# A transformer step on one core: the second branch's values as seven products of a pair, with the caches, the sums of x and the norm buffers moved

## The chip, the cores and the metric

The kernel runs on one core of a Trainium2 chip. The metric is the device time of one execution in microseconds (us), as the median of several runs. A core has five engines that run beside one another and meet through semaphores: TensorE (PE, matmuls and transposes), VectorE (DVE), ScalarE (ACT), GpSimd (POOL) and SyncE (SP, which here issues most DMA transfers). Each engine takes its instructions strictly in the order in which the program wrote them.

## The reference

One layer of a hybrid encoder, for 1024 prompt tokens and 64 sample tokens of width 1024, in float32:

```python
h = rms_norm(x, norm_w) @ w_in            # 6144 columns
sb_q, sb_k, sb_v, sb_z, cb_q, cb_k, cb_v, cb_z, g_sb, g_cb = split(h)
cb_q = rms_norm(cb_q per head, q_norm_w); cb_k = rms_norm(cb_k per head, k_norm_w)
o_sb = stick_breaking(sb_q, sb_k, sb_v)   # 8 heads x 64, all earlier keys
#   A[t,s] = beta[t,s] * prod_{s<j<t} (1 - beta[t,j]), beta = sigmoid(q.k/8)
o_cb = band_attention(cb_q, cb_k, cb_v, rel_bias)   # 8 heads x 64, a band of 512 and a bias
b_sb = (o_sb * silu(sb_z)) @ w_proj_sb;  b_cb = (o_cb * silu(cb_z)) @ w_proj_cb
y = x + (sigmoid(g_sb) * b_sb + sigmoid(g_cb) * b_cb) @ w_out
```

The sample tokens do the same against caches of 512 keys and values per branch. Beside y the kernel returns the new keys and values of both branches; of the second branch's prompt tokens, the last 512.

## The kernel before

Every float32 operand is split into a high part and a rest, both held in the rounded format F32R (`hi` and `lo` in the code). A product is three matmuls for each slice of 128 of the contracted dimension: high by high, rest by high, high by rest. ACT makes the high part as a copy, DVE or POOL the rest as a subtraction.

The projection by `w_in` comes first, in two stages.

The first stage (lines 202 to 577) works in natural layout, tokens on the partitions: for columns that need it, namely values (`sbv` from column 1024, `cbv` from 3072) and the second branch's queries and keys (from 2048 and 2560), which are normed per head. The list `NB` names eight blocks of 256 columns, `TO` the nine token tiles: the 64 sample tokens as tile 8 first, then tiles 0 to 7 of 128 tokens. The loop at line 492 takes block `i`, tile `ti`: 24 matmuls of 256 columns into an accumulator `acc` (16 for the sample tile, whose high part and rest lie side by side as 128 rows; `fold` adds the halves). Accumulators come from `psF` (two) and `psA` (one, every third tile). `evac_nat` empties one: for values ACT copies it to `vst`, which SP stores to the scratch `d_sbv` or `d_cbv` and to the output; for queries and keys ACT copies it to `qn` and squares it, DVE sums the squares and POOL raises them to a power (`rsqrt`), and a tile later `norm_nat` multiplies on DVE twice. `pend` holds normed tiles; when three wait, `post_nat` transposes the oldest on PE into the one PSUM tile `pk`, ACT makes its high part `hl`, DVE the rest.

Between the tiles of this loop stand, at places given as (block, tile), the other jobs. During the first block `ready` prepares x itself: `prep_s` (mean square), `prep_a` (`xn`, DVE), `prep_b` (transposes into `pt`, then `xa`, `xm`, `xb`). `W.split` makes the next block's weights: copy on ACT, subtraction on POOL (line 124); `load_nat` loads the ones after. `cache_load` loads a key cache into `ck`, and `cache_pair` transposes one of its four head pairs: four transposes on PE into the one PSUM tile `pc`, copy to `hc` on ACT, subtraction on DVE, one store of 512 KB to `d_csbT` or `d_ccbT`; `hc` has one buffer. `load_rb` loads the bias table into the buffer of `ck`, `make_rb` makes one head's reversed bias row `rx` on DVE and stores it to `d_rb`. `make_t` (line 162) makes four sums of x, four slices each, as 16 steps: two or three additions of 544 columns on DVE give `d`, then ACT copies and DVE subtracts (`put_t`).

The order on every engine is the one in which this code writes the instructions out; a pool that is closed gives its memory to the next one, whose first writes wait for the last readers, DMA reads among them.

The second stage (lines 582 to 732) takes the remaining columns in pairs of 128, tokens along the free dimension, by seven products for eight (Strassen's scheme in Winograd's form): two halves of x's tokens by two halves of its features against two by two weight quarters. It uses the sums of x from `make_t` (`tms`) and sums of weights from `presum`; `prep(n)` makes the weights of product n, copy on ACT and subtraction on POOL, five products ahead. Attention and the output follow and aren't touched by the change.

## Time and profile before

| | |
|---|---|
| Median of 3 runs (lowest to highest) | 967.85 us (967.75 to 968.23) |
| The profiled execution's own time | 967.6 us |
| Its span | 965.8 us |
| Busy: PE / DVE / ACT / POOL | 957.4 / 592.0 / 475.9 / 395.1 us |
| DMA traffic, mean rate | 175.76 MB, 182 GB/s |
| First matmul of the second stage | 226.6 us after the start |

A row of the timeline gives the start and the duration of an instruction in us, its engine, its line in the kernel, its operation, output and inputs, its shape, and in brackets how long its engine stood idle before it and what it then waited for. Groups give a count and durations in ns. A matmul's duration reaches from its issue to its end; matmuls overlap, so their pace is read from their starts or their count. A transfer's time to landing is from its issue on the queue to the arrival of its last byte.

### The profile page before, as it was taken

To read this page: it belongs to the slowest core of one execution; us is meant where nothing else is said; L and a number is where in the kernel's file an instruction comes from. 1 tells how busy PE (TensorE), PEld (TensorE's weight loads), DVE (VectorE), ACT (ScalarE), POOL (GpSimd) and SP (SyncE) were. 2 spreads that over 40 slices of the span, in tenths; PEclk is the share of its full clock that TensorE was granted. 3 is DMA by queue.
4 is the path that set the end of the run, shared out by engine and by line. 5 is a ranking of instruction groups with operands and counts; after the bars stand their busy time and mean duration, and the time that the engine had idled before them with its cause. 6 is when DMAs were issued, how large, how long until landed. Compare 5 with 4: busy or idle time off the path is not lost.

```text
span 965.8 us, 20494 instructions
## 1 busy us (share of the span) xinstructions
PE 957.4 (99%) x7645; PEld 912.3 (94%) x7645; DVE 592.0 (61%) x1170; ACT 475.9 (49%) x1054; POOL 395.1 (41%) x392
## 2 busy tenths in 40 slices
...
GB/s 222 233 81 243 196 222 249 180 95 132 188 136 185 173 196 152 173 182 151 179 87 86 283 259 209 190 165 250 230 302 251 248 111 77 262 197 70 208 151 75
DMA packets 173384, 175.76 MB, mean 182 GB/s; under 512 B 30745, under 2 KB 157597, under 8 KB 173158
## 3 DMA queue, kind: packets, MB, share of 16 engines
...
q0 software_dynamic: 2816, 6.69, 2.1%
...
## 4 chain that ended last, share of the span: by engine, by line
PE 97%; ACT 1%; DVE 1%; issue 0%; DMA 0%; POOL 0%; POOLq 0%; ACTq 0%
PE b L708 30%; PE acc L491 19%; PE b L1545 8%; PE o L1225 7%; PE z L1133 7%; PE pt L1186 7%; PE acc L984 5%; PE b L1026 5%; PE acc L877 5%; PE pk L352 1%; PE acc L1581 1%; PE pc L447 1%; PE pt L280 0%; DVE xn L269 0%; PE acc L633 0%; PE pc L374 0%
## 5 line engine op out<-in xcount | busy, mean ns | idle before, releaser
L1186 PE MATMUL pt<-ident,be 128*128 128x128 f32 (+1 forms) x568 | 87.8, 279 | 0.6 <-ACT wT L1195 0.2
L1155 DVE TENSOR_TENSOR_SCAN be<-be,imp 128x128 f32<-128x128 f32 (+7 forms) x64 | 83.4, 1343 | 8.1 <-ACT be L1136 7.9
L1133 PE MATMUL z<-ks,sq 128*128 128x320 f32 (+5 forms) x384 | 87.5, 338 | 0.0
L1186 PEld LDWEIGHTS pt<-ident,be 128*128 128x128 f32 (+1 forms) x568 | 65.7, 140 | 13.0 <-issue 4.6
L1195 ACT ACTIVATE wT<-pt 128x512 f32<-128x512 f32 (+3 forms) x123 | 56.9, 496 | 42.8 <-PE pt L1186 42.7
L491 PE MATMUL acc<-whi,xa 128*128 128x256 f32 x256 | 70.7, 291 | 0.3 <-ACT xa L288 0.3
L716 DVE TENSOR_TENSOR u<-b,s 128x256 f32<-128x256 f32 (+1 forms) x56 | 24.3, 440 | 75.4 <-PE b L708 72.0
L491 PE MATMUL acc<-wlox,xm 128*128 128x256 f32 x256 | 67.7, 280 | 0.0
L491 PE MATMUL acc<-whix,xm 128*128 128x256 f32 x256 | 67.6, 279 | 0.0
L491 PE MATMUL acc<-whi,xm 128*128 128x256 f32 x256 | 67.6, 279 | 0.0
L491 PE MATMUL acc<-wlo,xa 128*128 128x256 f32 x256 | 67.6, 279 | 0.0
L491 PE MATMUL acc<-whix,xb 128*128 128x256 f32 x256 | 67.5, 279 | 0.0
L1133 PEld LDWEIGHTS z<-ks,sq 128*128 128x128 f32 x384 | 63.7, 190 | 1.7
L1225 PE MATMUL o<-wT,vp 128*64 128x256 f32 (+1 forms) x608 | 64.2, 357 | 0.0
L1225 PEld LDWEIGHTS o<-wT,vp 128*64 128x64 f32 x608 | 40.3, 137 | 23.6 <-issue 7.4
L1158 ACT ACTIVATE be<-be,sm 128x640 f32<-128x640 f32 (+5 forms) x68 | 47.2, 694 | 17.0 <-DVE sm L1157 16.9
L124 POOL TENSOR_TENSOR wlo<-wraw,whi 128x1024 fp32r<-128x1024 f32 x15 | 35.9, 2397 | 44.3 <-ACT whi L117 40.8
...
L437 POOL TENSOR_TENSOR whix<-ws,whix 128x512 fp32r<-128x512 f32 x28 | 36.9, 1317 | 34.5 <-ACT whix L436 34.5
L1146 ACT ACTIVATE be<-be,sm 128x640 f32<-128x640 f32 (+5 forms) x68 | 47.3, 696 | 5.2 <-DVE sm L1138 4.8
L1136 ACT ACTIVATE be<-z 128x384 f32<-128x384 f32 (+6 forms) x104 | 47.9, 514 | 3.2 <-PE z L1133 2.4
L491 PEld LDWEIGHTS acc<-whi,xa 128*128 128x128 f32 x256 | 46.4, 188 | 0.7 <-ACT xa L288 0.5
...
## 6 DMA issues: line engine op xcount, KB each, us to landing
wraw<-in_w_in_dram SPq DMA_DIRECT2D x31, 512.0 KB, 4.2
wrawx<-in_w_in_dram SPq DMA_DIRECT2D x17, 512.0 KB, 4.6
...
xt<-in_x_prompt_dram SPq DMA_DIRECT2D x8, 512.0 KB, 4.9
d_kcbT<-hl SPq DMA_DIRECT2D x8, 512.0 KB, 4.3
d_qcbT<-hl SPq DMA_DIRECT2D x8, 512.0 KB, 3.1
...
```

Source lines behind the costliest of these rows:

```text
L491: TE.matmul(ps, x, w, start=first, stop=last)
L708: TE.matmul(ps[:, :m], w[:, hl_, k], right[s](x)[:, k, a:b], start=s < 3 and k == 0 and e == 0, stop=k == 3 and e == 2, skip_group_check=s ...
L877: TE.matmul(ps[:, :b - a], w[:, k], xk(x, k)[:, a:b], start=k == 0 and n == 0, stop=k == KT - 1 and n == 2)
L984: TE.matmul(ps[:, :e - a], w[:, p, cw], g[:, a:e], start=m % 12 == 0, stop=m % 12 == 11)
L1026: TE.matmul(pp[uu][:, :n], w[:, p, uu * 128:uu * 128 + 128], g[:, a:e], start=p == 0 and m == 0, stop=p == NPAIR - 1 and m == 2)
L1133: TE.matmul(z[:, :m], s[:, e, q0:q0 + 128], ks[:, h, o + x:o + y], start=(e, h) == parts[0], stop=(e, h) == parts[-1])
L1136: A.activation(be[:r, x:y], z[:r, :m], AF.Sigmoid, scale=-0.125)
L1155: V.tensor_tensor_scan(be[:r, n - 1::-1], be[:r, n - 1::-1], im[:, ::-1], 0.0, op0=OP.mult, op1=OP.max)
L1186: TE.transpose(pt[:kr, x, :r], be[:r, kb * 128:kb * 128 + kr], ident[:r, :r])
L1195: A.activation(w[:, sl:sl + m, q0:q0 + r], pt[:, :m, :r], AF.Copy)
L1225: TE.matmul(o[hd * 64:hd * 64 + 64, c0:c1], vv[:kr, kb, hd * 64:hd * 64 + 64], wT[b, p, j, hd, s // 4][:kr, s % 4, c0:c1] if j < 4 else wT ...
L1545: TE.matmul(ps[:, t], left[s](xs_, k)[:, ts_], wt_[:, k], start=s < 3 and t == k == e == 0, stop=k == 3 and e == 2, skip_group_check=s > 2 ...
```

## The change

The last two blocks of the first stage, `cbv` at columns 3072 and 3328, leave the list. They become one pair of a new part between the stages, in natural layout: seven products (`OPV`) of 512 x 512 tokens and features by 512 x 256 weights, each 2 x 24 matmuls, with the sums of x as the stationary side. `load_v_raw` loads four weight quarters, `v_sum` makes the four sums of weights, `prep_v` the weights of one product, `store_v` stores two tiles of results at once, and `sample_v` computes the 64 sample tokens as before.

The new part needs the sums of x, so their 16 steps move: from the last two blocks into every second tile of the third to sixth block. For that the memory of pool `p1` must be free by the end of the second block. So both caches are loaded in the first block (`ck` now with three buffers), their eight pairs are transposed in tiles 0 to 7 of the second block, one in each, the bias table is loaded in its first tile and the bias rows are made from its second tile on. The order of blocks becomes: both `sbv` blocks, then keys, then queries. The norm buffers (`qn`, `sqn`, `hl` and others) go to a pool of their own. Small changes beside: five idle transposes at the start for eight; the next weights are split a tile later in the first block, one half on DVE; transposes of x two matmuls sooner; the second pair product's weights are made after the new part.

The core of the diff:

```diff
+        nx = ExitStack()
+        p1b = nx.enter_context(tc.tile_pool(name="p1b", bufs=2, side="right"))
...
-        psA = ph.enter_context(tc.tile_pool(name="p1acc", bufs=1, space=PS))
-        psT = ph.enter_context(tc.tile_pool(name="p1tr", bufs=2, space=PS))
-        psK = ph.enter_context(tc.tile_pool(name="p1k", bufs=1, space=PS))
+        psA = nx.enter_context(tc.tile_pool(name="p1acc", bufs=1, space=PS))
+        psK = nx.enter_context(tc.tile_pool(name="p1k", bufs=1, space=PS))
+        psTx = ExitStack()
+        psT = psTx.enter_context(tc.tile_pool(name="p1tr", bufs=2, space=PS, side="right"))
...
-        NB = [1024, 2560, 2816, 2048, 2304, 1280, 3072, 3328]
+        NB = [1024, 1280, 2560, 2816, 2048, 2304]
...
-            rbs[0] = p1.tile([128, 8, 257], F32, name="ck", bufs=1)
+            rbs[0] = p1.tile([128, 8, 257], F32, name="ck", bufs=3)
...
-            qn = p1.tile([128, 4, 64], F32, name="qn", bufs=5)
+            sq = p1b.tile([128, 256], F32, name="sqn")
+            ms = p1b.tile([128, 4], F32, name="msn")
+            rs = p1b.tile([128, 4], F32, name="rsn", bufs=3)
+            qn = p1b.tile([128, 4, 64], F32, name="qn", bufs=5)
...
-                hl[0] = p1.tile([128, 2, 2, 576], F32R, name="hl", bufs=3)
+                hl[0] = p1b.tile([128, 2, 2, 576], F32R, name="hl", bufs=2)
...
-            ck = p1.tile([128, 4, 512], F32, name="ck", bufs=1)
+            ck = p1.tile([128, 4, 512], F32, name="ck", bufs=3)
...
-        beat(8)
+        beat(5)
...
+        OPV = [0, 3, 2, 1, 4, 5, 6]
+        OBV = {0: 1, 1: 2, 2: 3, 3: 1, 4: 2, 5: 2, 6: 3}
+
+        def load_v_raw(r, w):
+            pool, name, n = {(0, 0): (wpool, "wraw", 2), (1, 0): (wpool, "wraw", 2), (0, 1): (natx, "wrawx", 1),
+                             (1, 1): (natx, "whix", 2)}[r, w]
+            vraw[r, w] = pool.tile([128, 4, 256], F32, name=name, bufs=n)
+            c = 3072 + 256 * w
+            SP.dma_start(vraw[r, w], w_in[512 * r:512 * r + 512, c:c + 256].rearrange("(k p) n -> p k n", p=128))
+
+        def v_sum(n):
+            x, y, op, pool, name, bufs = {
+                2: ((0, 1), (1, 1), OP.add, natx, "wlox", 2), 1: (2, (0, 0), OP.subtract, natx, "wlox", 2),
+                4: ((0, 0), (0, 1), OP.subtract, natx, "whix", 2), 6: ((1, 0), 1, OP.subtract, None, "t6", 1)}[n]
+            d = vraw[n] = (pool or pv2).tile([128, 4, 256], F32, name=name, bufs=bufs)
+            V.tensor_tensor(out=d, in0=vraw[x], in1=vraw[y], op=op)
+
+        def prep_v(q):
+            s = OPV[q]
+            src = vraw[{0: (0, 0), 3: (1, 0), 5: (1, 1)}.get(s, s)]
+            h, l = (wpool.tile([128, 4, 256], F32R, name=x, bufs=2) for x in ("whi", "wlo"))
+            A.activation(h, src, AF.Copy)
+            G.tensor_tensor(out=l, in0=src, in1=h[:].bitcast(F32), op=OP.subtract)
+            vblk[q] = h, l
...
         def ready(j):
-            if 1 < j < 7:
+            if 2 < j < 7:
                 prep_a(j + 1)
             prep_b(j)
             if j == 0:
                 prep_s(1)
-            if j < 2:
+            if j < 3:
                 prep_a(j + 1)
...
-                    if i == 0 and m == (4, 20, 20, 16, 12, 8, 4, 0, -1)[ti]:
+                    if i == 0 and m == (4, 20, 18, 14, 10, 6, 2, 0, -1)[ti]:
...
-                if ti in (3, 6) and i > 0 or ti in (5, 6) and i == 0:
-                    h = 1 if ti == 6 else 0
+                if ti in (3, 6) and i > 0 or ti in (6, 7) and i == 0:
+                    h = 1 if ti == (6 if i else 7) else 0
                     if i + 1 < nb:
-                        W.split((i + 1, h))
+                        W.split((i + 1, h), V if i == 0 and h else None)
                     if i + 2 < nb:
                         load_nat(i + 2, h)
-                    elif h == 0:
-                        load_raw(i + 2 - nb)
-                if (i, ti) == (4, 2):
-                    load_rb()
-                if 0 <= 9 * i + ti - 40 < 8:
-                    make_rb(9 * i + ti - 40)
-                if i >= 5 and p1x is not None and not pend and not raw1 and ti >= 3:
+                    else:
+                        load_v_raw(*((0, 0), (1, 0), (0, 1), (1, 1))[2 * (i + 2 - nb) + h])
+                if (i, ti) in ((0, 5), (0, 8)):
+                    cache_load("sb" if ti == 5 else "cb")
+                if i == 1 and ti < 8:
+                    if ti == 0:
+                        load_rb()
+                    cache_pair("sb" if ti < 4 else "cb", ti % 4)
+                if 10 <= 9 * i + ti < 18:
+                    make_rb(9 * i + ti - 10)
+                if (i, ti) == (1, 0):
+                    psTx.close()
+                if (i, ti) == (1, 8):
                     p1x.close()
-                    p1x = None
                     tp = sx.enter_context(tc.tile_pool(name="tp", bufs=1))
                     pad(tp, 64)
                     tms = [[tp.tile([128, 4, HF], F32R, name=f"t{n}{s}") for s in "hl"] for n in range(4)]
-                    ws = sx.enter_context(tc.tile_pool(name="ws", bufs=3))
-                    tq = ph.enter_context(tc.tile_pool(name="tq", bufs=3))
+                    tqx = ExitStack()
+                    tq = tqx.enter_context(tc.tile_pool(name="tq", bufs=3))
                     tjobs = iter(make_t(tms, tq))
-                    tw = [3]
-                if p1x is None:
-                    tw[0] -= 1
-                    if tw[0] < 0:
-                        next(tjobs, None)
+                if i > 1 and (i + ti) % 2:
+                    next(tjobs, None)
                 if (i, ti) == (nb - 1, 5):
-                    prep(0)
-                if (i, ti) == (nb - 1, 6):
-                    presum(1)
-                if (i, ti) == (nb - 1, 7):
-                    prep(1)
-                if (i, ti) in ((0, 4), (2, 3)):
-                    cache_load("sb" if i == 0 else "cb")
-                at = {(1, 1): 0, (1, 4): 1, (1, 7): 2, (2, 1): 3}
-                if (i, ti) in at:
-                    cache_pair("sb", at[i, ti])
-                if (i - 2, ti) in at:
-                    cache_pair("cb", at[i - 2, ti])
+                    prep_v(0)
+                if (i, ti) == (nb - 1, 8):
+                    v_sum(2)
                 if (i, ti) in ((1, 1), (1, 5)):
...
+        tqx.close()
+        pvx = ExitStack()
+        pv = pvx.enter_context(tc.tile_pool(name="pv", bufs=2))
+        psV = ph.enter_context(tc.tile_pool(name="pvb", bufs=1, space=PS, side="right"))
+        leftv = [lambda e, k: xhl[e][0][:, k, 0:512], lambda e, k: tms[1][e][:, k, 0:512],
+                 lambda e, k: tms[0][e][:, k, 0:512], lambda e, k: xhl[e][1][:, k, 0:512],
+                 lambda e, k: tms[2][e][:, k, 0:512], lambda e, k: tms[3][e][:, k, 0:512],
+                 lambda e, k: xhl[e][1][:, k, HF:HF + 512]]
+        bank, sam, s1, u2, u3 = {}, {}, {}, {}, {}
...
+        def store_v(w, half, c, y):
+            a, cs = 512 * half + 256 * c, slice(256 * w, 256 * w + 256)
+            SP.dma_start(d_cbv[a:a + 256, cs].rearrange("(t q) n -> q t n", q=128), y)
+            if half:
+                SP.dma_start(o_cbv_p[a - 512:a - 256, cs].rearrange("(t q) n -> q t n", q=128), y)
+
+        def sample_v(w, r, blk_):
+            if r == 0:
+                sam[w] = psV.tile([128, 256], F32, name="sam")
+            for k in range(4):
+                for e, wt_ in enumerate(blk_):
+                    TE.matmul(sam[w], xs[:, 4 * r + k], wt_[:, k], start=r == k == e == 0, stop=r == 1 and k == 3 and e == 1)
+            if r == 1:
+                lo = fold(pn, sam[w])
+                v = pn.tile([128, 256], F32, name="vst", bufs=3)
+                A.activation(v[:64], lo, AF.Copy)
+                cs = slice(256 * w, 256 * w + 256)
+                SP.dma_start(d_cbv[NP:T, cs], v[:64])
+                SP.dma_start(o_cbv_s[:, cs], v[:64])
...
+        for q, s in enumerate(OPV):
+            if q < 6:
+                prep_v(q + 1)
+            else:
+                prep(0)
+            if q == 0:
+                v_sum(1)
+            if q == 3:
+                load_raw(0)
+                pb["b"] = pv2.tile([128, 4, 256], F32R, name="bh", bufs=1), pv2.tile([128, 4, 256], F32R, name="bl", bufs=1)
+                A.activation(pb["b"][0], vraw[0, 1], AF.Copy)
+                G.tensor_tensor(out=pb["b"][1], in0=vraw[0, 1], in1=pb["b"][0].bitcast(F32), op=OP.subtract)
+            if q == 5:
+                load_raw(1)
+            wh, wl = vblk.pop(q)
+            for c in range(2):
+                if s < 3:
+                    bank[OBV[s], c] = (psF.tile([128, 2, 256], F32, name="acc") if s == 0 else
+                                       (psV if s == 2 else psW).tile([128, 2, 256], F32, name=f"v{OBV[s]}{c}"))
+                ps = bank[OBV[s], c]
+                for t in range(2):
+                    ts_ = slice((2 * c + t) * 128, (2 * c + t) * 128 + 128)
+                    for k in range(4):
+                        for e, (x_, wt_) in enumerate(((0, wh), (1, wh), (0, wl))):
+                            TE.matmul(ps[:, t], leftv[s](x_, k)[:, ts_], wt_[:, k], start=s < 3 and t == k == e == 0,
+                                      stop=k == 3 and e == 2, skip_group_check=s > 2 or t > 0)
+                if s == 0:
+                    s1[c] = pv.tile([128, 2, 256], F32, name="s1")
+                    A.activation(s1[c], ps, AF.Copy)
+                    if c == 0:
+                        if raw1:
+                            norm_nat(*raw1)
+                            pend.append(raw1[:3])
+                elif s == 3:
+                    y = pv.tile([128, 2, 256], F32, name="y")
+                    A.activation(y, ps, AF.Copy)
+                    store_v(0, 0, c, y)
+                elif s == 1:
+                    u2[c] = pv2.tile([128, 2, 256], F32, name="u2")
+                    V.tensor_tensor(out=u2[c], in0=ps, in1=s1[c], op=OP.add)
+                elif s == 4:
+                    u3[c] = pv2.tile([128, 2, 256], F32, name="u3")
+                    V.tensor_tensor(out=u3[c], in0=ps, in1=s1[c], op=OP.add)
+                    V.tensor_tensor(out=u3[c], in0=bank[3, c], in1=u3[c], op=OP.add)
+                    store_v(1, 1, c, u3[c])
+                elif s in (5, 6):
+                    y = s1[c] if s == 5 else u2[c]
+                    V.tensor_tensor(out=y, in0=ps, in1=y, op=OP.add)
+                    store_v(*((1, 0) if s == 5 else (0, 1)), c, y)
+                if q < 2:
+                    for _ in range(2):
+                        if pend and (q or c):
+                            post_nat(*pend.pop(0))
+            if s in (0, 3):
+                sample_v(0, s // 3, (wh, wl))
+            elif s == 5:
+                sample_v(1, 1, (wh, wl))
+            elif s == 4:
+                sample_v(1, 0, pb["b"])
+            if q == 1:
+                assert not pend
+                nx.close()
+                pb = {}
+                pv2 = ph.enter_context(tc.tile_pool(name="pv2", bufs=2, side="right"))
+                psW = ph.enter_context(tc.tile_pool(name="pvw", bufs=1, space=PS))
+            if q == 2:
+                v_sum(4)
+            if q == 4:
+                v_sum(6)
+        pvx.close()
+    ws = sx.enter_context(tc.tile_pool(name="ws", bufs=3))
...
         load_raw(2)
-        for n in range(2, LEAD):
+        presum(1)
+        for n in range(1, LEAD):
             prep(n)
             presum(n + 1)
```

9 lines of the change are left out of this document (4 added, 5 removed).

## The prediction

> **What bounds the kernel now.** I read the page's head first, then the chain of work that ended last, then the windows of the first 220 us, where the change lies.
>
> ```profile
> span 965.8 us, 20494 instructions
> PE 957.4 (99%) x7645; PEld 912.3 (94%) x7645; DVE 592.0 (61%) x1170; ACT 475.9 (49%) x1054; POOL 395.1 (41%) x392
> PE 97%; ACT 1%; DVE 1%; issue 0%; DMA 0%; POOL 0%; POOLq 0%; ACTq 0%
> ```
> TensorE is busy 99% of the span and makes 97% of the chain, so a matmul fewer is time gained, and any new wait of PE is time lost: nothing later has room to give it back. Windows (span of the stretch, PE, PEld, DVE, ACT and POOL busy with counts, clock, DMA share, GB/s):
>
> ```profile
> 97.00:122.00 25.00, 25.00 (x216) 24.80 (x215) 16.79 (x37) 10.80 (x29) 15.62 (x20) 1.00 0.55 190
> 172.00:197.00 25.00, 25.00 (x218) 25.00 (x217) 18.08 (x24) 9.05 (x18) 4.80 (x2) 1.00 0.51 163
> ```
> What counts of matmuls is not the duration of one but the pace. 218 matmuls in 25 us are 0.115 us each. A tile of 24 takes 2.76 us, and a block of 208 matmuls about 24 us. That is the yardstick for everything that another engine must do per tile.
>
> **The change, part by part.**
>
> *Fewer products.* Two blocks of the second branch's values go: 2 x (8 x 24 + 16) = 416 matmuls 256 wide. Seven products come: 7 x 2 x 24 = 336, and for the sample 2 x 16 = 32. 416 - 368 = 48 fewer x 0.115 = **-5.5 us**. This is the whole gain that the change can promise on PE.
>
> *The start.* Now PE waits once in the first block:
>
> ```profile
> 37.87 1.25 PE L280 MATMUL pt<-ident,xn 128*128 128x128 f32 x8 [1.36 <-DVE xm L289]
> 33.65 3.56 DVE L269 SCALAR_TENSOR_TENSOR xn<-xt,rs,nw 128x512 f32<-128x512 f32 x2 [0.63 <-POOL rs L252]
> 30.41 1.41 DVE L269 SCALAR_TENSOR_TENSOR xn<-xt,rs,nw 128x512 f32<-128x512 f32 x2 [0.62 <-POOL rs L252]
> 34.27 2.40 POOL L124 TENSOR_TENSOR wlo<-wraw,whi 128x1024 fp32r<-128x1024 f32 x1 [0.66 <-ACT whi L117]
> 33.14 1.05 ACT L117 ACTIVATE whi<-wraw 128x1024 fp32r<-128x1024 f32 x1
> ```
> The two `xn` instructions take 3.56 us in place of 1.41, because a POOL subtraction of 2.40 us runs into them. The change splits the next weights one tile later, behind the last `xn`, and does the second half on DVE: **-1.4 us**, at the least 0, where that subtraction now meets the last `xm` subtraction. The fewer idle beats I cost at nothing: the sample's `xn` ends as they end now. Transposes that come two matmuls (0.23 us) sooner, loads from the weights' queue and `nw8`'s new pool: nothing, the arrivals don't change. Norm buffers in another pool, `hl` with two buffers for three: nothing, a buffer's store is issued five tiles (14 us) before the next use. That covers `psK` and `psA` in their new pool too: they are closed a product before their space is written.
>
> *The caches, the term that decides.* Now one cache pair is transposed every third tile or so. The change does one in each of the first eight tiles of the second block, with the same single buffers `pc` and `hc`. The answer on `hc`, min/median/max, and the landing of its store:
>
> ```profile
> L376 ACT ACTIVATE hc<-pc x8: 607/620/620, 49.9 to 132.4; 128x512 fp32r<-128x512 f32 x8
> L377 DVE TENSOR_TENSOR hc<-pc,hc x8: 673/678/687, 51.2 to 133.7; 128x512 fp32r<-128x512 f32 x8
> DMA to landing us min/median/max: 2.6/3.9/5.2
> 49.17 0.60 PE L374 MATMUL pc<-ident,ck 128*128 128x128 f32 x4
> 49.53 0.37 PE L491 MATMUL acc<-whi,xa 128*128 128x256 f32 x1
> 49.73 0.28 PE L491 MATMUL acc<-whi,xm 128*128 128x256 f32 x1
> 46.54 0.38 ACT L295 ACTIVATE fl<-acc 64x256 f32<-64x256 f32 x1 [1.49 <-PE acc L491]
> 47.40 0.42 ACT L322 ACTIVATE qn<-fl 64x256 f32<-64x256 f32 x1 [0.48 <-DVE fl L296]
> ```
> Four transposes cost PE 49.53 - 49.17 = 0.36 and some 0.08 on the next matmul, so an unhindered tile is 2.76 + 0.44 = 3.2 us. But `hc` can only be rewritten when its store has landed: ACT 0.62, DVE 0.68, about 0.1 of handover, landing L. The period is P = 1.4 + L: 4.0, 5.3 or 6.6 us for L of 2.6, 3.9, 5.2. PE's next four transposes need `pc`, which DVE frees at the end of each period; the matmuls between cannot run further ahead. The first pair is through DVE 2.75 us after the sample tile (fold 46.54 to 47.82, then 0.62 + 0.68, handovers), the eighth transposes come six periods later, against 7 x 3.2 = 22.4 us unhindered: the stall is 2.75 + 6P - 22.4 = 4.3, 12.2 or 20 us. I take the median landing, **+12.2 us**. The bytes say the same: stored bias rows, loads and values share that queue.
>
> ```profile
> d_csbT<-hc SPq DMA_DIRECT2D x4, 512.0 KB
> d_rb<-rx SPq DMA_DIRECT2D x8, 384.0 KB, 3.7
> d_sbv<-vst SPq DMA_DIRECT2D x16, 128.0 KB, 3.1
> ck<-in_rel_bias_dram SPq DMA_DIRECT2D x1, 1028.0 KB
> ck<-in_cache_sb_k_dram SPq DMA_DIRECT2D x1, 1024.0 KB, 8.0
> GB/s 336 393 369 276 234 329 254 197 344 0 119 401 4 0 22 0 0 0 70 153 243 377 410 408 411 381 396 382 400 378 412 361 403 363 389 356 310 76 225 270
> ```
> Eight pairs (4.2 MB), eight bias rows (3.1), values stored twice (2.2), the second cache and the biases (2.1), two weight halves (1.0): 12.7 MB in a block of 24 + 8 x 0.44 = 27.5 us. The last line (140 to 170 us in 40 slices) holds some 390 GB/s at its best; 12.7 MB at that are 32.5 us. Behind the waiting `hc` copy on ACT stand the evacuations, behind a late bias row on DVE the `hc` subtraction, on SP all stores in order; PE has three accumulators against it, two to three tiles. The bias load is now issued one tile before its first use; at 8.0 us to landing it comes about when the second pair leaves DVE (2.75 + 5.3), so it hides behind that, and costs DVE 5 us if the pairs don't wait. The first `d` in the third block waits for the last `hc` store: some 2 us of DVE, counted below.
>
> *Sums of x among the norm blocks.* They stood in the last two blocks, where DVE had no norm. Now they come in every second tile of four norm blocks.
>
> ```profile
> 65.08 0.38 ACT L356 ACTIVATE hl<-pk 128x256 fp32r<-128x256 f32 x1 [2.04 <-PE pk L352]
> 65.50 0.42 DVE L357 TENSOR_TENSOR hl<-pk,hl 128x256 fp32r<-128x256 f32 x1 [1.21 <-ACT hl L356]
> 66.06 0.42 DVE L324 TENSOR_REDUCE msn<-sqn 128x4 f32<-128x256 f32 x1
> 66.39 0.41 DVE L332 TENSOR_TENSOR qn<-qn,rsn 128x256 f32<-128x256 f32 x1
> 66.84 0.42 DVE L333 TENSOR_TENSOR qn<-qn,wqk 128x256 f32<-128x256 f32 x1
> 66.94 1.19 POOL L252 TENSOR_TENSOR rsn<-rsn,half 128x4 f32<-128x4 f32 x1
> 183.25 0.72 DVE L176 TENSOR_TENSOR d<-xm,d 128x544 f32<-128x544 f32 x1
> 185.28 0.72 DVE L169 TENSOR_TENSOR d<-xm,xa 128x544 f32<-128x544 f32 x1
> 188.08 0.72 DVE L169 TENSOR_TENSOR d<-xa 128x544 f32<-128x544 f32 x1
> 190.92 2.49 DVE L158 TENSOR_TENSOR t2l<-d,t2h 128x544 fp32r<-128x544 f32 x1 [0.61 <-ACT t2h L157]
> 190.42 2.40 POOL L124 TENSOR_TENSOR wlo<-wraw,whi 128x1024 fp32r<-128x1024 f32 x1 [13.46 <-ACT whi L117]
> ```
> By the starts a norm tile costs DVE 1.5 us, a short sum 185.28 - 183.25 = 2.03, a long one 188.08 - 185.28 = 2.80, 2.4 on the mean. Four blocks: 36 x 1.5 + 4 x 0.4 (fold) + 16 x 2.4 = 94 us, and 1 to 1.8 us more wherever DVE meets a POOL weight subtraction (2.49 in place of 0.72), seven of them: 104 us. PE needs 226 / 216 x 25 = 26.2 us a block, 104.6 in all. DVE is full, in order, and holds PE by the single `pk`: the next transposes wait for `hl`. Without further loss the uneven blocks cost 2 to 5 us. But the first `d` of a sum follows L333 at once, just as POOL's power (1.19 us) runs; if DVE is held there as by the weights, 17 x 0.9 = 15 us come on top, less the slack of a tile: up to 16. No row has the two together, so the ends are 0 and 16, and I take the middle, **+8 us**. [...]
>
> *The product stage.* A product lasts PE 48 x 0.115 = 5.5 us; its weights need ACT 1.05 and POOL 2.40, and a sum on DVE, an estimated 1.36 (1024 / 544 x 0.72): 4.8 in all, hidden, with about a microsecond to spare before the last product, whose sum stands behind two adds. Evacuations of 512 columns (0.62) hide in the 2.76 of the next half product; the stores and the later raw loads hide too, the buffers' last readers being a product back. But the four last norm tiles are transposed two and two in a row with one `pk`: each second one waits for the 512-column copy 0.6, `hl` 0.38, subtraction 0.42 and handovers, 1.6 us, twice: **+3.2 us** (0 to 4).
>
> *Into the pairs.* The second block of pair weights was made in the last tiles; now two sums, its copy and its subtraction begin after the last product:
>
> ```profile
> 224.37 0.69 DVE L404 TENSOR_TENSOR ws<-ws,wraw 128x512 f32<-128x512 f32 x1
> 227.12 0.62 ACT L436 ACTIVATE whix<-ws 128x512 fp32r<-128x512 f32 x1
> 227.82 1.30 POOL L437 TENSOR_TENSOR whix<-ws,whix 128x512 fp32r<-128x512 f32 x1 [0.71 <-ACT whix L436]
> 226.59 0.28 PE L708 MATMUL b<-xa,whi 128*128 128x256 f32 x1
> 229.60 0.28 PE L708 MATMUL b<-t1h,wlo 128*128 128x256 f32 x1
> ```
> 0.7 (last evacuation) + 2 x 0.69 + 0.62 + 1.30 + handovers = 4.2 us; the first product covers 229.60 - 226.59 = 3.0. **+1.2 us** (0 to 2). Behind that, attention and the end are untouched.
>
> *Sum:* -5.5 - 1.4 + 12.2 + 8 + 3.2 + 1.2 = +17.7. The profiled execution took 967.6 us (span 965.8), the median of the runs is 967.85; 967.6 + 17.7 = 985.3, **985 us**.
>
> **The rivals.**
> - *PE's lead swallows the waits.* The three stalls all pass through a transpose's single PSUM tile; if PE doesn't see them there, 967.6 - 6.9 + 1.2 = **962 us**, faster. It decides when they total under 3.8 us. Against it: the 1.36 us row is just such a wait, and the caches alone make 4.3 at the shortest landing; they vanish only at L under 1.9 us. Chance 0.13.
> - *DVE held at every power.* The sums cost 16: 985 + 8 = **993 us**. For it the 2.49 us row; against it that these POOL instructions touch four columns. Chance 0.22.
> - *Stores land as late as the latest now.* L = 5.2, stall 20: **993 us**. For it the volume; against it that a stalled block stretches the time for it. Chance 0.15.
>
> **How the numbers follow.** My forecast, with both long terms at their middle or less, has 0.5, of which 0.05 lies at its foot, all stalls at their low ends: 967.6 - 6.9 + 4.3 = 965. Its own range is 969 to 990: the caches at 4.3 give 977, the sums at 0 beside that 969, and 5 us of the two bound terms more 990. The two slow rivals have 0.37, 993 each and 1001 together. So 964 to 1001 leaves out most of the fast rival and little above. What a measurement tells from no change is 0.2%, 1.9 us: faster 0.13, within it 0.05 (that foot), slower 0.82.
>
> **What would show it.** In the profile after: PE waiting at L374's line on DVE `hc`, and ACT `hc` on its own store, in the second block, which lasts near 40 us; no 1.36 us wait in the first; DVE nine tenths busy through the four norm blocks with PE waiting at `pk` on `hl`; 48 matmuls fewer. The prediction is wrong if PE keeps its 216 instructions per 25 us there.

## The result and the profile after

The changed kernel takes 999.35 us (median of 4 runs, 994.24 to 1001.5). Beside it the kernel before took 968.04 us (967.75 to 969.7). The ratio is 1.031, with a 95% interval of 1.029 to 1.033. The forecast was 985 us with a range of 964 to 1001. It had the sign right, the time lay inside its range, and it was 14 us short.

The profiled execution took 1000.77 us. The page of the changed kernel, its span, its TensorE line and the head of its chain:

```profile
span 999.0 us, 20386 instructions
PE 964.0 (96%) x7591; PEld 915.0 (92%) x7591; DVE 606.2 (61%) x1185; ACT 475.2 (48%) x1046; POOL 403.9 (40%) x395
PE 82%; DVE 8%; DMA 4%; ACT 3%; issue 1%; POOL 1%; SPq 0%; ACTq 0%; DVEq 0%; POOLq 0%
```

There are 54 matmuls fewer in the records, yet PE is busy for longer. Its share of the chain fell from 97% to 82%, and DVE, DMA and ACT have the rest. That PE is *busier* with less to do is the first hint that its clock has changed.

Now the windows view (stretch, its length, PE, PEld, DVE, ACT and POOL busy with counts, granted clock, DMA share, GB/s). First the kernel before, from its second block to the first pair product, where everything runs at pace:

```profile
44.42:226.59 182.17, 182.17 (x1562) 181.36 (x1561) 121.87 (x235) 73.06 (x180) 85.62 (x94) 1.00 0.52 174
```

Then the changed kernel: its second block with the caches, its four norm blocks, its product stage, and the 25 us that answer to those shown of before:

```profile
42.78:84.84 42.06, 31.46 (x242) 30.86 (x241) 9.97 (x22) 9.73 (x19) 5.99 (x6) 0.88 0.74 251
84.84:208.20 123.36, 111.65 (x899) 109.39 (x897) 103.92 (x198) 49.51 (x130) 69.60 (x76) 0.94 0.37 123
208.20:257.56 49.36, 45.27 (x380) 44.63 (x377) 19.05 (x29) 13.85 (x23) 20.97 (x12) 0.97 0.39 126
97.00:122.00 25.00, 19.75 (x145) 19.16 (x144) 20.55 (x39) 8.12 (x22) 15.53 (x16) 0.86 0.18 58
```

The row of before gives the pace: 182.17 / 1562 = 0.1166 us for a matmul. At that pace the three stages would last 242 x 0.1166 = 28.2, 104.8 and 44.3 us. They last 42.1, 123.4 and 49.4: they lose 13.8, 18.5 and 5.0 us. Fewer matmuls give back (1562 - 1521) x 0.1166 = 4.8 (the code has 48 fewer; some records are missing), and the stretch starts 44.42 - 42.78 = 1.6 sooner. From the first pair product to the end the new kernel takes 999.0 - 257.56 = 741.4 us against 965.8 - 226.59 = 739.2, another 2.2 lost. Together that makes 13.8 + 18.5 + 5.0 + 2.2 - 4.8 - 1.6 = 33.1, which is the difference of the spans, 33.2. In the last row 145 matmuls stand where the kernel before has 216.

What PE waited for, in the first 300 us of the changed kernel (releaser, total us, times, the longest):

```profile
PE pk L355 <- DVE hl L360: 14.9, 9, 3.7
PE pc L377 <- DVE hc L380: 10.6, 3, 7.8
PE pt L283 <- DVE xn L272: 0.9, 2, 0.7
PE b L832 <- DVE u L677: 0.9, 1, 0.9
```

`pk` and `pc` are the two single PSUM tiles of the forecast; the `pt` row is two short waits at 7.4 and 8.0 us, where fewer idle transposes stand, and the one wait of 1.36 us in the first block is gone. Two of the nine waits on `pk`, 2.01 and 1.20 us, stand in the product stage. So the waits are 10.6 us in the second block, 11.7 in the norm blocks, and 2.0 + 1.2 + 0.9 = 4.1 in the product stage and at the pairs. That is 26.4 us, against 24.6 forecast for these three places. But the stages lost 37.3. The windows at the right places show the remainder:

```profile
56.00:62.80 6.80, 3.60 (x17) 3.60 (x18) 1.47 (x4) 1.47 (x3) 0.00 (x0) 0.50 0.52 195
73.10:76.50 3.40, 3.06 (x15) 3.06 (x16) 0.82 (x3) 0.35 (x1) 0.00 (x0) 0.50 0.69 272
103.80:110.60 6.80, 6.03 (x29) 6.03 (x29) 5.40 (x12) 1.48 (x4) 2.98 (x4) 0.50 0.01 2
148.20:151.60 3.40, 3.40 (x19) 3.40 (x18) 3.16 (x8) 1.48 (x4) 3.11 (x4) 0.51 0.74 260
182.30:185.70 3.40, 3.40 (x18) 3.40 (x17) 2.54 (x8) 2.03 (x5) 1.98 (x4) 0.50 0.75 261
216.40:219.80 3.40, 3.40 (x17) 3.40 (x18) 0.42 (x1) 1.44 (x2) 0.12 (x1) 0.50 0.01 2
```

In six stretches, 27.2 us together, the granted clock is 0.50. In the kernel before it is 1.00 over the stretch from 7 us to the end. What half clock does to the pace shows in the fourth stretch and just behind it:

```profile
150.71 0.41 PE L519 MATMUL acc<-whix,xs 128*128 128x256 f32 x1
150.92 0.41 PE L519 MATMUL acc<-wlox,xs 128*128 128x256 f32 x1
152.74 0.28 PE L519 MATMUL acc<-wlo,xa 128*128 128x256 f32 x1
152.86 0.28 PE L519 MATMUL acc<-whi,xa 128*128 128x256 f32 x1
```

The starts lie 0.213 us apart at half clock (all fifteen from 148.36 to 151.35) and 0.118 at full clock, so the pace is 1.8 times slower and not twice. PE was busy for 22.9 us of the six stretches, and 1 - 0.118 / 0.213 = 45% of that, 10.2 us, is lost: 3.0 in the second block, 5.7 in the norm blocks, 1.5 in the product stage. Waits and half clock add up stage by stage: 10.6 + 3.0 = 13.6 (13.8 lost), 11.7 + 5.7 = 17.4 (18.5), 4.1 + 1.5 = 5.6 (5.0). So two causes make nearly all of the loss: waits, as forecast, and a clock that falls to half behind the longer ones, which the forecast didn't have.

Where the longest waits come from, in rows of the changed kernel's timeline. First the cache pairs: ACT's copies to `hc`, and the queue ahead of the first store.

```profile
44.28 0.50 SPq L371 DMA_DIRECT2D ck<-in_cache_cb_k_dram  x1
48.19 0.59 SPq L244 DMA_DIRECT2D ck<-in_rel_bias_dram  x1
48.88 0.41 SPq L51 DMA_DIRECT2D d_csbT<-hc  x1
57.83 0.60 ACT L379 ACTIVATE hc<-pc 128x512 fp32r<-128x512 f32 x1 [9.26 <-DMA d_csbT<-hc]
61.92 0.60 ACT L379 ACTIVATE hc<-pc 128x512 fp32r<-128x512 f32 x1 [3.22 <-DMA d_csbT<-hc]
65.99 0.60 ACT L379 ACTIVATE hc<-pc 128x512 fp32r<-128x512 f32 x1 [0.30 <-DMA d_csbT<-hc]
72.07 0.60 ACT L379 ACTIVATE hc<-pc 128x512 fp32r<-128x512 f32 x1 [4.06 <-DMA d_csbT<-hc]
101.46 2.86 DVE L158 TENSOR_TENSOR t0l<-d,t0h 128x544 fp32r<-128x544 f32 x1
100.99 2.75 POOL L124 TENSOR_TENSOR wlo<-wraw,whi 128x1024 fp32r<-128x1024 f32 x1
104.57 0.69 PE L355 MATMUL pk<-ident,qn 128*128 128x128 f32 x2 [3.67 <-DVE hl L360]
123.78 0.72 DVE L169 TENSOR_TENSOR d<-xa 128x544 f32<-128x544 f32 x1
123.55 1.18 POOL L255 TENSOR_TENSOR rsn<-rsn,half 64x4 f32<-64x4 f32 x1
```

The first store was issued at 48.88, behind two loads of 1 MB each on the same queue. ACT could rewrite `hc` at 57.83, almost 9 us later. After that the copies follow one another at 4.1 us (57.83, 61.92, 65.99), which is the forecast's P with a landing of 2.6, and after 6.1 where a 512 KB weight load stood ahead on the queue. The last five rows are the sums. A DVE subtraction that meets POOL's weight subtraction takes 2.86 us in place of 0.72, and PE waits 3.67 us for the `hl` behind it. The POOL power at 123.55, however, doesn't hold the DVE addition that starts 0.23 us into it: 0.72 us. All sixteen first additions of a sum start while such a power runs, and all take 0.71 to 0.73.

### The profile page after: what moved, and what is told of

Its sections match the earlier page's. It is cut to its first block, busy times and chain, and to the rows that moved or that the text cites. A ratio compares the mean times of both kernels' runs of the same rounds, so it can differ in the third digit from the quotient of the medians.

```text
span 999.0 us, 20386 instructions
## 1 busy us (share of the span) xinstructions
PE 964.0 (96%) x7591; PEld 915.0 (92%) x7591; DVE 606.2 (61%) x1185; ACT 475.2 (48%) x1046; POOL 403.9 (40%) x395
## 4 chain that ended last, share of the span: by engine, by line
PE 82%; DVE 8%; DMA 4%; ACT 3%; issue 1%; POOL 1%; SPq 0%; ACTq 0%; DVEq 0%; POOLq 0%
PE b L832 29%; PE o L1349 7%; PE acc L519 7%; PE z L1257 7%; PE pt L1310 7%; PE b L1669 6%; PE acc L1108 5%; PE acc L1001 5%; PE b L1150 4%; PE v L654 3%; DMA d_csbT<-hc 2%; DVE qn L335 1%; DMA d_ccbT<-hc 1%; PE pt L283 1%; PE pk L355 1%
## 5 line engine op out<-in xcount | busy, mean ns | idle before, releaser
L519 PE MATMUL acc<-whi,xa 128*128 128x256 f32 x192 | 55.6, 309 | 0.2 <-ACT xa L291 0.2
L124 POOL TENSOR_TENSOR wlo<-wraw,whi 128x1024 fp32r<-128x1024 f32 x13 | 32.0, 2458 | 49.3 <-ACT whi L117 46.1
L519 PE MATMUL acc<-whi,xm 128*128 128x256 f32 x192 | 51.9, 290 | 0.0
L519 PE MATMUL acc<-wlo,xa 128*128 128x256 f32 x192 | 51.8, 289 | 0.0
L519 PE MATMUL acc<-whix,xm 128*128 128x256 f32 x192 | 50.6, 283 | 0.0
L519 PE MATMUL acc<-whix,xb 128*128 128x256 f32 x192 | 50.4, 282 | 0.0
L519 PE MATMUL acc<-wlox,xm 128*128 128x256 f32 x192 | 50.3, 282 | 0.0
L440 POOL TENSOR_TENSOR whix<-ws,whix 128x512 fp32r<-128x512 f32 x28 | 36.9, 1317 | 32.5 <-ACT whix L439 28.2
L440 POOL TENSOR_TENSOR wlo<-ws,wlo 128x512 fp32r<-128x512 f32 x28 | 39.5, 1412 | 18.1 <-ACT wlo L439 17.9
```

Source lines behind the costliest of these rows:

```text
L440: G.tensor_tensor(out=t[:, 1], in0=src, in1=t[:, 0].bitcast(F32), op=OP.subtract)
L519: TE.matmul(ps, x, w, start=first, stop=last)
```

## The experiments

All times are medians; ratios are against the kernel before, run beside each, which took 967.1 to 967.8 us. Unless another base is named, an experiment edits the changed kernel.

**The caches: a second buffer for `hc`.**

```diff
-            h = p1.tile([128, 2, 512], F32R, name="hc", bufs=1)
+            h = p1.tile([128, 2, 512], F32R, name="hc", bufs=2)
```

> The changed kernel with two buffers hc for one, nothing else. My theory: the eight cache pairs wait for the store of the pair before, so with two buffers the period falls from about 4 to 8 us to half of that, under the 3.2 us of a tile; only the first stores, behind 2 MB of loads, still hold PE for some 5 us. The second block (42.1 us in the changed kernel, from 42.8 to 84.8) lasts 31 to 34 us and the kernel 988 to 992 us. Rival, the bytes: 12.7 MB don't pass in that block whatever the buffers; ACT and DVE then wait for the bias rows' and values' buffers instead, the block stays at 39 us or more and the kernel at 996 to 1000 us.

Measured: 988.93 us (988.52 to 990.88), ratio 1.023 (1.021 to 1.024), 10.4 us less than with one buffer. The time is in the theory's range; the second block, 35.8 us for 42.1, is above the theory's 31 to 34 and below the rival's 39. One wait on `pc` is left, 4.9 us, since the third pair still needs the first store. So the store-to-rewrite chain is the cause of the 6.3 us gained in this block. The rest fell elsewhere: the norm blocks took 119.0 us for 123.4 and the product stage 48.0 for 49.4, though PE waited on `pk` no less (15.6 us for 14.9). They had no half clock in this execution. So that part isn't shown to come from the buffer; the runs on the clock below bear on it.

**The caches: the three big loads sooner.**

```diff
-                if (i, ti) in ((0, 5), (0, 8)):
-                    cache_load("sb" if ti == 5 else "cb")
+                if (i, ti) in ((0, 3), (0, 5)):
+                    cache_load("sb" if ti == 3 else "cb")
+                if (i, ti) == (0, 7):
+                    load_rb()
```

(and the old place of `load_rb` in the second block goes.)

> The changed kernel with its three 1 MB loads issued sooner: the first key cache in tile 3 of the first block for tile 5, the second in tile 5 for tile 8, the bias table in tile 7 for the first tile of the second block. Nothing else moves. Theory: the first store from hc landed 8.9 us after its issue because two such loads stood ahead of it on SP's queue; with them gone it lands in about 4, PE's first wait on pc falls from 7.84 us to 3 or less, its stretch at half clock goes, and the second block lasts 36 to 38 us for 42.1: 991 to 994 us. Rival: the period of hc (copy, subtraction, landing) alone sets the block, as the forecast's 6P has it; then the wait only moves to later pairs, the block keeps 40 us or more and the run 997 to 1000.

Measured: 994.52 us (991.94 to 995.14), ratio 1.027 (1.026 to 1.029). The landing of the stores from `hc`, and what PE waits for, in this kernel's answers:

```profile
DMA to landing us min/median/max: 2.6/2.6/5.6
PE pc L377 <- DVE hc L380: 6.1, 2, 3.3
```

The changed kernel's own answer to the first:

```profile
DMA to landing us min/median/max: 2.6/2.6/8.8
```

The longest landing fell from 8.8 to 5.6 us, the first wait from 7.84 to 3.3, the block from 42.1 to 37.6. The theory's wait of 3 at most and its "about 4" were a little low, half clock still follows that wait, for 3.4 us in place of 6.8, and the time is half a us above the theory's range. The rival, the period alone, is refuted: the waits on `pc` fell from 10.6 to 6.1 us and did not move to later pairs.

**The sums: POOL's weight subtraction moved to DVE in the norm blocks.**

```diff
-                        W.split((i + 1, h), V if i == 0 and h else None)
+                        W.split((i + 1, h), V if i or h else None)
```

> The changed kernel with the weights' subtraction of the norm blocks on DVE for POOL. Theory hold: DVE is late at the transposes because a 544-wide instruction with two SBUF inputs stands still while POOL subtracts weights (2.86 us for 0.72 at 101.5 us, ahead of PE's 3.7 us of idle). DVE's own subtraction costs 1.2 us and no hold, so the four norm blocks (123.4 us in the changed kernel) fall to 112 to 116 us, the clock keeps its full rate there, and the kernel takes 987 to 993 us. Rival load: DVE is simply full, the 1.2 us a piece come on top of it; the norm blocks stay at 121 to 126 us and the kernel at 997 to 1002 us.

Measured: 988.46 us (986.44 to 990.48), ratio 1.022 (1.020 to 1.023). The four norm blocks of this kernel in one window:

```profile
84.57:197.30 112.73, 106.25 (x896) 103.90 (x894) 98.41 (x204) 49.59 (x130) 54.48 (x69) 1.00 0.38 127
```

112.7 us for 123.4, the clock 1.00 throughout, and DVE is busy for less time (98.4 for 103.9) though it has more to do. So the meeting of the two engines costs more than the work that it hides. Of the 10.7 us the shorter waits make 5.2 (6.5 on `pk` for 11.7) and the half clock 5.7; whether half clock never follows waits like those left, 1.84 and 1.54 us, this run doesn't show. 7.9 us above the pace of 104.8 are left.

**The sums: left out.** The additions of `make_t` and its remainders are left out; ACT copies slices of x into the same tiles, so the values of the second branch are not the reference's.

```diff
-            for got in sums_of(k):
-                if held:
-                    put(*held)
-                held = got
+            for n in range(4):
+                for s in range(2):
+                    A.activation(tm[n][s][:, k], x(s, n // 2, k, n % 2), AF.Copy)
                 yield
```

> The changed kernel with the additions and subtractions of the sums of x left out: ACT alone writes the same tiles as copies of x, so the outputs that need them are not the reference's; the number of matmuls is the same. Both theories of the norm blocks: without the sums on DVE their four blocks take 26.5 to 27.5 us each, 106 to 110 for 123.4, and the kernel 983 to 987 us. If the time of these blocks comes from elsewhere (queries and keys in a row, the buffers of the norm pool), they stay over 115 us and the kernel over 992 us.

Measured: 980.6 us (978.07 to 981.2), ratio 1.013 (1.012 to 1.015), better than expected. The four norm blocks of this kernel:

```profile
86.10:190.64 104.54, 104.54 (x899) 103.74 (x897) 64.50 (x143) 58.08 (x146) 68.20 (x77) 1.00 0.42 140
```

PE has no idle time here. So the whole loss of the norm blocks comes from the sums on DVE, and none from the moved norm buffers or the new order of blocks.

**The product stage: one `post_nat` after each half product.**

```diff
-                if q < 2:
-                    for _ in range(2):
-                        if pend and (q or c):
-                            post_nat(*pend.pop(0))
+                if q < 3 and pend and (q or c):
+                    post_nat(*pend.pop(0))
```

(and the memory of the norm buffers is given on a product later.)

> The changed kernel with the four last norm tiles transposed one for each half product (three products instead of two), not two in a row. Theory: the two waits at the second transposes (2.0 and 1.2 us) go, and the stretch at half clock behind them (3.4 us): the product stage, 49.4 us from 208.2 to 257.6 in the changed kernel, falls by 3 to 5 us and the kernel takes 994 to 997 us. Rival: DVE is still behind from the norm blocks when the stage begins, the same waits stand at the single transposes, and the kernel stays at 998 to 1001 us.

Measured: 991.61 us (990.25 to 992.97), ratio 1.025 (1.023 to 1.026), below the theory's range: 7.7 us gained where 3.2 us of waits and at most 1.5 of half clock went. The two waits are gone from this stage, which lasts 44.3 us for 49.4, as the theory had it. The rest is not this stage's: the profiled execution has 10.2 us at half clock where the changed kernel's has 27.2, though three of the norm blocks' waits ahead of it are as long as they were (1.55, 1.87 and 2.77 us for 1.58, 1.95 and 2.78). The same waits, not followed by the same half clock: that asked for an experiment on the clock itself.

**The price of a wait: six of them put into the kernel before.** They stand where PE had none, each a chain of copies on ACT that two transposes need; nothing reads the transposes.

```diff
+                if i > 5 and ti % 3 == 2:
+                    z = psK.tile([128, 2, 128], F32, name="pk")
+                    for k in range(2):
+                        TE.transpose(z[:, k], ident, ident)
+                    wt = pn.tile([128, 2, 128], F32, name="wt", bufs=1)
+                    for _ in range({8: 2, 11: 5, 14: 8, 17: 4, 20: 6, 23: 10}[9 * (i - 6) + ti + 6]):
+                        A.activation(wt, z, AF.Copy)
+                    z = psK.tile([128, 2, 128], F32, name="pk")
+                    for k in range(2):
+                        TE.transpose(z[:, k], wt[:, k], ident)
```

> The kernel before, with six waits put into its seventh and eighth block, where PE had none: after tiles 2, 5 and 8 two transposes, then a chain of copies of 128 x 256 on ACT (2, 5 and 8 in the seventh block, 4, 6 and 10 in the eighth), and two transposes that need the last of them. Nothing reads the last transposes; the outputs are the reference's. At some 0.35 us a copy and 0.4 of handovers the waits should be 1.1, 2.15, 3.2, 1.8, 2.5 and 3.9 us, 14.7 in all, and the transposes 2.2. Theory: a PE wait of about 2 us or more is followed by 3.4 to 6.8 us at half clock, a shorter one is not; then four of the six are, at 1.7 to 3.4 us each, and the run takes 992 to 998 us. Rival: the half clock in the changed kernel had another cause; then nothing but the waits is paid, the clock stays at 1.0 and the run takes 983 to 987.

Measured: 993.46 us (991.58 to 995.48), ratio 1.028 (1.026 to 1.029), so the theory's range holds. Three waits, not four, are followed by half clock: those of 3.45, 2.61 and 4.28 us, and not those of 0.89, 1.78 and 2.20. The timeline's rows for the two at the border:

```profile
198.26 0.44 PE L526 MATMUL pk<-ident,wt 128*128 128x128 f32 x2 [2.20 <-ACT wt L523]
233.81 0.44 PE L526 MATMUL pk<-ident,wt 128*128 128x128 f32 x2 [2.61 <-ACT wt L523]
```

What decides is not the length alone: the wait of 2.20 us here was not followed by half clock, the changed kernel's waits of 1.95 and 2.01 us were. All starts of half clock in this execution lie whole multiples of 3.413 us apart (211.13, 235.02, 248.67), and so do those of the changed kernel (55.99, 73.06, 103.78, 148.15, 182.29, 216.42). Laid on that grid, windows of this kernel show, for the waits of 2.20, 3.45, 1.78 and 2.61 us, the window with most of the wait and then the next:

```profile
194.06:197.48 3.42, 2.00 (x18) 1.76 (x16) 3.35 (x6) 1.22 (x4) 0.00 (x0) 1.00 0.13 44
197.48:200.89 3.41, 2.63 (x23) 2.63 (x24) 2.35 (x4) 1.52 (x4) 0.00 (x0) 1.00 0.25 78
207.71:211.13 3.42, 0.59 (x5) 0.60 (x6) 2.30 (x4) 3.23 (x9) 0.00 (x0) 1.00 0.00 0
211.13:214.54 3.41, 3.41 (x18) 3.41 (x17) 0.72 (x1) 0.50 (x2) 0.00 (x0) 0.50 0.25 79
217.95:221.37 3.42, 2.33 (x20) 2.09 (x19) 3.32 (x6) 1.18 (x4) 0.00 (x0) 1.00 0.12 38
221.37:224.78 3.41, 2.72 (x23) 2.72 (x24) 2.54 (x4) 1.42 (x4) 0.00 (x0) 1.00 0.14 43
231.60:235.02 3.42, 1.21 (x11) 1.21 (x12) 0.83 (x2) 3.26 (x9) 0.00 (x0) 1.00 0.04 13
235.02:238.43 3.41, 3.41 (x19) 3.41 (x18) 0.32 (x1) 0.08 (x1) 1.30 (x1) 0.50 0.20 66
```

Where PE was busy for 0.59 or 1.21 us of a window, the next ran at 0.50. Where it was busy for 2.00 or 2.33, the clock stayed. The wait of 2.20 us was cut in two by the grid, 1.41 and 0.79. Closer together lie the next windows. The first row below is the changed kernel ahead of its stretch at 148.2, the next two the kernel with two `hc` buffers, on its own grid:

```profile
144.74:148.15 3.41, 1.46 (x14) 1.26 (x12) 3.41 (x5) 0.00 (x0) 1.53 (x1) 1.00 0.17 41
```

```profile
137.37:140.79 3.42, 1.59 (x14) 1.59 (x15) 3.34 (x8) 1.12 (x4) 1.37 (x3) 1.00 0.51 150
140.79:144.20 3.41, 3.41 (x31) 3.41 (x31) 3.21 (x7) 1.13 (x3) 1.97 (x3) 1.00 0.82 284
```

1.46 us busy of 3.41 was followed by half clock, 1.59 wasn't. In two other kernels it was the other way round. Below, on their own grids, are two windows of the fifth version of the better order that follows, where 1.59 us busy was followed by half clock, and two of the kernel without the sums, where 1.49 wasn't:

```profile
190.60:194.01 3.41, 1.59 (x14) 1.40 (x13) 2.74 (x3) 2.66 (x5) 3.08 (x1) 1.00 0.46 154
194.01:197.43 3.42, 3.42 (x18) 3.42 (x18) 0.78 (x1) 0.00 (x0) 2.96 (x1) 0.50 0.59 169
```

```profile
72.77:76.18 3.41, 1.49 (x13) 1.49 (x14) 1.23 (x3) 0.87 (x2) 0.00 (x0) 1.00 0.47 174
76.18:79.59 3.41, 2.71 (x24) 2.52 (x24) 1.23 (x3) 1.93 (x3) 0.06 (x1) 1.00 0.72 267
```

In the changed kernel, from 40 us to the first pair product, the windows at full clock that were followed by half clock had 0.00, 1.21, 0.53, 1.46, 0.64 and 1.40 us busy (from 52.58, 69.65, 100.37, 144.74, 178.87 and 213.01); of the others the least busy had 1.84 (from 117.43). What decides between such values isn't shown, and the ends of matmuls, from which busy time is counted, are modelled. So in these traces the price of a wait depended on where it fell on the grid: the 2.20 us of this kernel, in windows with 2.00 and 2.63 us busy, cost no half clock, the 1.95 us of the changed kernel, in one with 1.46, brought 3.41 us of it. The four runs of the kernel with six waits agree with that: the same instructions took 991.58, 993.11, 993.81 and 995.48 us at mean clocks of 0.995, 0.995, 0.993 and 0.991.

**The three edits together**: two `hc` buffers, the weight subtraction on DVE, one `post_nat` at a time.

> Three edits together: two buffers hc, the weights' subtraction of the norm blocks on DVE, single transposes in the product stage. Theory: three separate waits, each with its own place, so their gains add: 999.4 - 10.4 - 10.9 - 3 to 5 = 973 to 976 us. Rival: one wait covers the other (DVE's backlog or the half clock is shared between them), the gains overlap by half, and the kernel takes 980 us or more.

Measured: 975.81 us (974.38 to 978.55), ratio 1.009 (1.007 to 1.011), within the theory's range. But the gains don't add, as the theory had it: the single ones were 10.4, 10.9 and 7.7 us, which would make 970.3. Each of the three edits had taken most of the same half clock away (27.3 us of it in the changed kernel's trace, 6.8, 10.2 and 10.2 in theirs, 3.4 in this one), so it can't be counted three times. In that the rival was right, though not in its size.

**A better order.** The same seven products, with the caches in every third tile again (from the second block to the fourth), the bias rows between them, the second `sbv` block last, where there is no norm, and the sums of x in the last two blocks and the first products. The core of the edit (the places of the loads, the bias rows and the memory pools move with it):

```diff
-        NB = [1024, 1280, 2560, 2816, 2048, 2304]
+        NB = [1024, 2560, 2816, 2048, 2304, 1280]
...
+                if g in range(10, 32, 3):
+                    cache_pair(*(("sb", "cb")[(g - 10) // 12], (g - 10) // 3 % 4))
...
-                if i > 1 and (i + ti) % 2:
+                if i == 4 and ti in (0, 2, 5, 7, 8) or i == 5:
```

> The seven products kept, but the caches spread as before (a pair every third tile of blocks 2 to 4), the bias rows between them, the second value block of the first branch put last, and the sums of x made in it, in five tiles of the block before and in the first two products; pool of the next stage's weight sums opened early, so that its second weights are ready in time. My theory: no stall is left of the three, so the kernel gains the 48 matmuls (5.5 us), the 1.6 us of the start, and loses at most 1 to 2 us: 960 to 964 us. Rival: the product stage itself costs more than it saves (49.4 us in the changed kernel for 368 matmuls, 42.3 us by the pace) through its weights and evacuations; then that stage stays over 46 us and the kernel at 966 us or more.

Measured: 970.25 us (968.39 to 971.86), ratio 1.0024 (1.0014 to 1.0035): a miss of 6 us, and both signs of the rival are there: the product stage lasts 46.6 us, and the kernel is above 966. Nearly all of the loss is gone, but PE still waits 2.5 us in two waits on a product's weights, 3.3 on `pk` and 0.9 at the first pair product.

The next version set the pairs in every second tile with two `hc` buffers, three sums each in the fourth and the fifth block, the fifth block's weight subtractions on DVE, and the first pair product in free PSUM tiles. Its core, against the version before:

```diff
-                if g in range(10, 32, 3):
+                if g in range(10, 26, 2):
...
-                if i == 4 and ti in (0, 2, 5, 7, 8) or i == 5:
+                if i in (3, 4) and ti in (1, 5, 8) or i == 5:
```

> The spread kernel with its last waits taken out: pairs every second tile of blocks 2 and 3 with two buffers hc, the bias rows in block 3, so that the sums of x may begin in block 4: three in each of blocks 4 and 5, in tiles in which POOL subtracts no weights, nine in the value block, two beside the first product; the last weights' subtraction on DVE; the first pair product in PSUM tiles that are free. The spread kernel stood 6.7 us still in pk (3.3), weights of the second and third product (2.5) and the first pair product (0.9). Theory: all go, 962 to 965 us, faster than the kernel before. Rival: DVE has only so much room in those blocks; the waits move to the earlier blocks and the kernel stays at 967 to 971 us.

Measured: 966.69 us (965.71 to 969.01), ratio 0.9992 (0.9983 to 1.0001), between the two ranges. One longer wait, 1.92 us, is left on a product's weights, followed by 3.4 us at half clock, and one of 1.0 on `pk`. Four edits of this version went after it:

```diff
-            if q == 0:
+            if q == 1:
                 v_sum(1)
...
-                if i in (3, 4) and ti in (1, 5, 8) or i == 5:
+                if i in (3, 4) and ti in (1, 5, 8) or (i, ti) == (3, 7) or i == 5:
...
-                if q == 0:
+                if q == c == 0:
                     next(tjobs, None)
```

(and, as the fourth, the rest of the second product's weights on DVE.)

> The spread2 order with four edits against its one wait of 1.9 us and the stretch at half clock behind it: a sum's step more in the fourth block and one fewer in the first product, the sum of weights for the fourth product made a product later, and the rest of the second product's weights made on DVE, so that POOL doesn't hold DVE there. Theory: the wait of 1.9 us and 1.7 us of half clock go, nothing takes their place, and spread2's 966.7 becomes 962 to 964. Rival: DVE is so full in the last block of this stage that the step that goes from the first product is paid by a wait on pk in the fourth block: 965 to 967.

Measured: 967.38 us (965.86 to 968.65), ratio 0.9997 (0.9988 to 1.0006), no gain. The rival's mechanism held: the half clock is gone, but `pk` waits 3.2 us behind the added step and a product 1.6 us for its weights from DVE.

The fourth version sets the steps at even distances:

```diff
-                if i in (3, 4) and ti in (1, 5, 8) or i == 5:
+                if (i, ti) in ((3, 0), (3, 2), (3, 5), (3, 8), (4, 1), (4, 5), (4, 8)) or i == 5:
```

(with the first and the last of the edits shown for the version before; the second product's weights are back on POOL.)

> The spread2 order with the sum of weights for the fourth product made a product later, and the steps of the sums of x set at even distances: four in the fourth block (tiles 0, 2, 5, 8) for three, three in the fifth (1, 5, 8) as before, one in the first product for two. Theory: what cost spread2 its one wait of 1.9 us was DVE's queue in the first product (two sums of weights of 1.2 us and the last sum of x) and what cost spread3 its pk waits was two steps in tiles 7 and 8; with both gone the run takes 962 to 964 us. Rival: DVE has no room for a fourth step in a norm block wherever it stands; pk waits of 2 to 4 us remain there and the run takes 965.5 to 967.5.

Measured: 966.15 us (965.35 to 969.07), ratio 0.9988 (0.9980 to 0.9997). The rival's mechanism held here too. What PE waits for after the first block, and the stretch from the second block to the first pair product:

```profile
PE pk L355 <- DVE hl L360: 3.7, 3, 1.8
43.03:223.96 180.93, 177.12 (x1515) 175.10 (x1513) 131.46 (x250) 73.53 (x173) 92.50 (x95) 1.00 0.52 176
```

The fifth is the second with one edit, `v_sum(1)` a product later:

```diff
-            if q == 0:
+            if q == 1:
                 v_sum(1)
```

> The spread2 order with one edit: the sum of weights for the fourth product is made a product later. It takes 1.2 us from DVE's queue ahead of the last sum of x, so the copy of the third product's weights on ACT starts 1.2 us sooner. Theory: the 1.9 us wait falls under 1 us, the stretch at half clock behind it goes, and 966.7 becomes 963.5 to 965. Rival: POOL's subtraction of those weights, which holds DVE or is held by it, takes the gain up again: 966 to 967.5.

Measured: 966.5 us (963.91 to 968.75), ratio 0.9985 (0.9977 to 0.9994). The rival held: the copy of the third product's weights starts 1.35 us sooner (189.50 for 190.85 us), but POOL's subtraction behind it, which now meets the moved sum of weights, takes 3.08 us for 2.35, and the wait of 1.92 us is still 1.8, with its half clock.

So the seven products can be had a little faster than the kernel before, by 0.12 to 0.15% in the last two of five versions (their intervals end 0.03 and 0.06% below the kernel before), and no more was found. The pair products start at 223.96 us for 226.59. Of the 6.9 us that fewer products and an earlier start should bring (5.5 + 1.4), 3.7 go to `pk`, and after the first pair product this kernel takes 964.3 - 223.96 = 740.3 us against 739.2; the spans differ by 1.5.

## Why the prediction was right, and where it fell short

By its own steps, from the profiled execution:

| step | forecast us | measured us |
|---|---|---|
| fewer products | -5.5 | -4.8 by the records |
| the start | -1.4 | -1.6 |
| caches, waits on `pc` | +12.2 | +10.6 |
| sums, waits on `pk` in the norm blocks | +8 | +11.7 |
| product stage, waits on `pk` | +3.2 | +3.2 |
| into the pairs | +1.2 | +0.9 |
| half clock behind the waits | not in it | +10.2 |
| from the first pair product on | 0 | +2.2 |

*The step that failed is the price of a wait.* The forecast took each wait at its length. In the changed kernel six waits, of 7.84, 2.58, 3.67, 1.95, 2.78 and 2.01 us, left PE busy for 0.00 to 1.46 us of a 3.413 us window, and each time the next window ran at 0.50; behind the first and the third, where that window had 3.20 and 0.79 us of idle time itself, another one did. That made 10.2 of the 15.5 us by which the profiled execution (1000.77) stands above the sum of 985.3. The profile before doesn't show it: from 40 us to its last matmul PE was never idle there for more than 0.22 us.

*The caches*: the place and the mechanism were right (PE on `pc`, ACT on its own store). The size came out near by two errors against each other. The median landing was 2.6 us and not 3.9, which by the forecast's own sum is 2.75 + 6 x 4.0 - 22.4 = 4.4 us. The first landing was 8.8, 6.2 above it, and 4.4 + 6.2 is 10.6. The sentence that the bias load "hides behind" the pairs had it the wrong way round: the load didn't come late for the bias rows, it stood ahead of the first store. With the loads sooner, the waits fell by 4.5 us.

*The sums*: DVE's work was forecast at 104 us and is 103.9, though spread over 123 us that is 84% and not the nine tenths named. The middle of 0 and 16 was taken because the power on POOL might hold DVE. That doubt is settled: it doesn't (0.72 us beside a power of 1.18). Beside a weight subtraction of 1024 columns a DVE subtraction took 2.86 us. What was under-priced is the meetings with the seven weight subtractions. Three of them meet an instruction of a sum (2.79 to 2.92 us for 0.72), four a multiplication of the norm (1.44 to 2.61 for 0.41). The forecast counted 1 to 1.8 us each as DVE work, but such a meeting can delay the one `hl` that PE needs, and half clock can follow: behind the 2.86 us from 101.46 PE waited 3.67 us and ran 6.8 us at half clock, behind the 2.79 us from 144.06 it waited 1.95 and ran 3.4 so. With the subtractions on DVE the norm blocks lose 7.9 us; that this is near the forecast's 8 is chance, for the 8 was the middle of two ends. Without the sums they lose nothing.

*The product stage and the pairs* came out as worked out: two waits at `pk` (2.01 and 1.20 for twice 1.6) and 0.88 at the first pair product for 1.2.

*The rivals.* PE's lead did not swallow the waits. DVE is not held at every power, though that rival's 993 lies nearer to the result than 985; its time was nearer for another reason. Stores did not land as late as 5.2 throughout: the median was 2.6, with one at 8.8. So that the time lay inside the range is in part luck: its upper end, 1001, stood for both slow rivals at once, neither came, and the half clock took their place.

*What stays open.* The rows of the table add up to 32.4 us of the 33.2 between the spans. The last 2.2 us fall late: 1.0 while the `og` products run, some 604 to 651 us behind the first pair product, and 1.2 about 670 to 690 us behind it, where PE waits 0.6 us on a weight remainder from POOL (L1150). No run was made on it. The spread of the changed kernel's four runs, 994 to 1001 us, is argued and not shown to be the grid's phase. The kernel with six waits, which has its spread in the same order as its clock, speaks for it; the changed kernel's own runs do so only roughly (1001.5 us at 0.990, 1000.77 at 0.986, 997.93 and 994.24 both at 0.995).
